# A hybrid decoder block on one core: two value projections and a gate column join pairs that take seven products for eight

## The chip, the cores and the metric

The kernel runs on one core of one Trainium2 chip. The metric is device time in microseconds of one execution. Before the change three runs gave 1403.35, 1406.06 and 1406.92 us; the median, 1406.06 us, is the time before.

## The reference, cut to what matters

One decoder layer on a sequence of 256 tokens with 2048 channels, in float32:

```python
h = rmsnorm(x, g_mix)
proj = h @ w_in                      # 256 x 2048 by 2048 x 12288
q, k, v = ...                        # 16 heads of 128 columns each
gates = sigmoid(proj[..., 3 * MIX_WIDTH:])
o_a = stick_breaking_attention(q[:, :4], k[:, :4], v[:, :4])
qn = rmsnorm(q[:, 4:], q_gain); kn = rmsnorm(k[:, 4:], k_gain)
o_b = moba_attention(qn[:, :6], kn[:, :6], v[:, 4:10], rel_bias[:, :6])
o_c = dilated_attention(qn[:, 6:], kn[:, 6:], v[:, 10:], rel_bias[:, 6:])
merged = gates[0] * (o_a @ w_branch[:512]) + gates[1] * (o_b @ ...) + gates[2] * (o_c @ ...)
x = x + merged @ w_out
gu = rmsnorm(x, g_ffn) @ w_gu
return x + (silu(gu[..., :5632]) * gu[..., 5632:]) @ w_down
```

The change touches the columns of `w_in` for v and for one gate, and the norms and attentions that lie among those projections. The sixteen heads are worked in four groups of four: group 0 is the stick-breaking one, groups 1 to 3 are softmax groups with a norm on q and k.

## The kernel before, in words

**Products.** Every float32 matmul of a projection is made from three float32r products of a high and a low part (`product`, lines 174 to 178): high by high, high by low, low by high. So each 128 x 1024 block of weights is split once: ACT casts it to `w_hi`, DVE subtracts that from the block and writes `w_lo` (`split`, line 110). `w_hi` and `w_lo` have five buffers each; the blocks arrive by DMA in four buffers `w_raw` and six `g_raw`.

**Units.** The first projection is worked as a list of units, each of one or two column blocks of 512. A plain unit (`project`) takes 16 row blocks by 2 token tiles by 3 products, that is 96 matmuls and 8 splits. A pair (`project_pair`) computes two column blocks at once. For half of the rows (the chunks `WC`) it uses seven block products where eight would do (Strassen-Winograd: sums of blocks of the activations are made beforehand, sums of blocks of the weights, `u` and `g_raw`, are made on DVE at lines 320 and 331), and for the other half it works plainly. That makes 180 matmuls, 22 splits, 8 sums of blocks on DVE, four copies of intermediate results out of PSUM on ACT (`snapshot`, line 315) and four 128 x 512 sums on DVE that give the results (lines 375, 377, 380, 389). A form of the seven takes six products from each split, a plain step twelve.

**Order.** The units before are v0, gate, qk0, qk1, v1, qk2, v2, qk3, v3, gate, and then five pairs of gate columns. The qk units and the gate pairs are pairs; v0 to v3 and two gate columns are plain. Everything else lies among them as generators that are advanced step by step: `stages` at each split, `slow_stages` at each second one. `rows_to_columns` squares q and k with sums per row on ACT (line 663, 16 per group), makes the inverse root on DVE and ACT, scales the rows on DVE (line 681), and turns them: groups 0 to 2 by PE transposes, group 3 by DMA transposes issued from ACT between two copies (lines 650, 652 and 673). `attention` then runs two pairs of heads per group; for a softmax pair the scores (lines 591, 593) go to DVE and ACT for the softmax, come back to PE as transposes (618 to 620), are copied to `pT` on ACT (621), and meet v on PE (628, 629); ACT copies the result out (544). `keep_v` finishes all slow stages before it takes the single buffer of v, so one group's attention has to end before the next v.

The kernel's instructions pass through a scheduler that orders each engine's queue by its own estimate of time; a step given to `keep_in_program_order` keeps its place among the others so marked. Each engine then runs its queue in that order.

**Later work.** After the group attentions the pool of the attention is closed, two further PSUM banks come free for the pairs (`acc2`, `beside`), and the attention's output is split (`split_o`) at four given places. Branch projections, output projection, the two products of the feed-forward part follow.

Of the kernel before, what the change touches and what calls it, by code (L numbers as in the profile page):

```python
# [18 lines left out]
P = 128  # L19
# [38 lines left out]
def hybrid_block(ctx: ExitStack, tc: tile.TileContext, x, w_in, w_branch, w_out, w_gu, w_down, rel_bias, xT, gains,  # L58
# [132 lines left out]
            nc.vector.tensor_scalar(t, t, -0.5, 1.5, op0=ALU.mult, op1=ALU.add)  # L191
            nc.vector.tensor_mul(dst if it else y, y, t)

    def transpose4(src):

        pt = tr.tile([P, 4, P], F32, name="tr")
        for i in range(4):
            nc.tensor.transpose(pt[:, i, :], src[:, i * P:(i + 1) * P], ident)
        return pt


# [454 lines left out]
    def rows_to_columns(g, sbs, dst):  # L656
        if g:
            ss = pa.tile([P, 4 * NT * 2], F32, name="ss", bufs=1)
            for i, sb in enumerate(sbs):
                junk = half_kb()  # L660
                for hd in range(4):
                    cols = slice(hd * HD, (hd + 1) * HD)
                    nc.scalar.activation(junk[:, cols], sb[:, cols], AF.Square,
                                         accum_out=ss[:, 4 * i + hd:4 * i + hd + 1])
                yield
            rr = pa.tile([P, 4 * NT * 2], F32, name="rr", bufs=1)
            rsqrt_mean(rr, ss, HD, 4 * NT * 2)
            yield
        def join(d, turned, j):
            joined.append(j)  # L670
            if j == 0 and g:
                turned = turned[..., ::-1]
            tc.keep_in_program_order(nc.scalar.copy(d.bitcast(U16).rearrange("p k (q b) -> p b k q", b=2), turned))
            if j == 0 and g:
                hs = 4 * g - H_A
                nc.vector.tensor_mul(d, d, gq[:, hs:hs + 4, None].to_broadcast([P, 4, P]))

        for i, sb in enumerate(sbs):
            if g:
                sb3 = sb.rearrange("p (h d) -> p h d", h=4)  # L680
                nc.vector.tensor_mul(sb3, sb3, rr[:, 4 * i:4 * i + 4, None].to_broadcast([P, 4, HD]))
                yield
            j, t = divmod(i, NT)
            if g not in (3,):
                pt = transpose4(sb)
                d = dst[j][:, :, t * P:(t + 1) * P]
                if j:
                    nc.scalar.copy(d, pt)
# [12 lines left out]

    def until_joined(g):
# [26 lines left out]
    heads = {}  # L729

    def keep_v(g, ps):
        if g:
            finish_stages(slow_stages)
        heads["v", g] = v = pa.tile([P, NT, NB], F32, name="v", bufs=1)

        def scaled():
            for t in range(NT):
                nc.scalar.activation(v[:, t, :], ps[t], AF.Copy, scale=rstd[:, t:t + 1])
            yield

        if g:
            finish_stages([scaled()])
            slow_stages.append(until_joined(g))
            slow_stages.append(attention(g, *heads["qk", g], v))
        else:
            stages.extend((first_norm(), scaled()))

    def keep_qk(g, q0, q1, k0, k1):
        sbs = []
# [8 lines left out]
        if g:  # L758
            stages.append(rows_to_columns(g, sbs, qkT))
        else:  # L760
            slow_stages.append(rows_to_columns(g, sbs, qkT))
            slow_stages.append(attention(g, *qkT, heads["v", g]))

    chunks = [(c, b) for c in range(4) for b in range(3)]
# [6 lines left out]
    def pair_of(kind, what):  # L773
        if kind == "qk":
            return hs, w_in, what * NB, NH * HD + what * NB
        if kind == "gates":
            return hs, w_in, gate_col(*what[0]), gate_col(*what[1])

    def in_turn():
        turn.reverse()  # L780
# [8 lines left out]
    others = in_turn  # L789
    ahead = None  # L790
    for (kind, what), after in zip(units, units[1:] + [(None, None)]):
        if kind == "gates" and what[0] == chunks[4]:
            finish_stages(slow_stages)
            pat.close()
            acc2 = ctx.enter_context(tc.tile_pool(name="acc2", bufs=1, space=PSUM))
            others = beside
            o = Columns(pool(ph1, "o", "left"), "o", NH)
            for i in range(NH // 4):
                at_split[split_count[0] + 22 * i + 12] = [lambda k=4 * i: split_o(k)]
        nxt = pair_of(*after)  # L800
        if kind in ("qk", "gates"):
# [7 lines left out]
        finish_stages(stages)  # L809
        if kind == "v":  # L810
            keep_v(what, ps)
        elif kind == "qk":
            keep_qk(what, *ps)
        elif kind == "gate":
            keep_gate(*what, ps)
        else:
# [336 lines left out]
```

## Time and profile before

| | |
|---|---|
| median of three runs | 1406.06 us (1403.35 to 1406.92) |
| span of the profiled execution | 1402.7 us |
| PE busy | 1394.4 us, 99%, 6197 instructions |
| DVE busy | 1208.7 us, 86%, 1290 instructions |
| ACT busy | 959.1 us, 68%, 1204 instructions |
| weight loads of PE busy | 1150.2 us, 82% |
| HBM traffic | 220 GB/s over the span |

The profiled execution's own time is its span, 1402.7 us from the first to the last instruction; the runs' times contain what lies around that, and their median is 3.4 us longer. Engines are PE (matmul), PEld (its weight loads), DVE, ACT, POOL and SP. A matmul's end is modelled: a matmul of 512 columns is shown with about 0.39 us but the next one starts about 0.227 us later, so that a wait of PE under some 0.16 us does not show as idle time.

### The profile page before, as it was taken

The numbers are of one execution on the slowest core, as the hardware profiler recorded it, in microseconds if no ns is written. First come the engines' busy times: TensorE is split into PE (matmuls) and PEld (weight loads), VectorE is DVE, ScalarE is ACT, GpSimd is POOL, SyncE is SP. The second block draws the span as 40 slices with busy tenths as digits, with TensorE's granted clock in tenths as the row PEclk, the third lists the DMA queues.
The fourth block names the chain that finished last, engine by engine and source line by source line (L and its number), as shares of the span: only waits on it lengthen the run. The fifth ranks groups of instructions, "written<-read, shape, count | busy, mean of one in ns | idle before, by whom it ended". The sixth has DMA issues, their size and how long they took to land. (4 is left out here: it accounts for less than half of the span.)

```text
span 1402.7 us, 17407 instructions
## 1 busy us (share of the span) xinstructions
PE 1394.4 (99%) x6197; PEld 1150.2 (82%) x6197; DVE 1208.7 (86%) x1290; ACT 959.1 (68%) x1204; POOL 20.1 (1%) x45
## 2 busy tenths in 40 slices
PE   9999999999999999999999999999999999999998
PEld 7888888888888888888878888888888888788887
DVE  6997887857899997875789999999999998997887
ACT  7777867787767675666767677776776776754553
POOL 1000000000000000000000000000000000000000
PEclk9999999999999999999999999999999999999999
DMA  9764647684657667998876766677877779877562
GB/s 341 277 225 125 235 123 251 182 228 137 235 202 246 223 200 264 326 278 243 263 232 239 225 205 222 205 210 250 250 234 240 231 226 307 281 239 260 196 198 87
DMA packets 208967, 320.56 MB, mean 229 GB/s; under 512 B 53064, under 2 KB 65376, under 8 KB 208880
## 3 DMA queue, kind: packets, MB, share of 16 engines
q1 hardware_dynamic: 153216, 293.64, 62.8%
q10 hardware_dynamic: 53136, 17.86, 6.6%
q0 software_dynamic: 2528, 7.95, 1.5%
q8 instruction: 48, 0.79, 0.2%
q14 instruction: 39, 0.32, 0.1%
HBM read 294.22 MB, written 14.70 MB: 220 GB/s over the span
## 5 line engine op out<-in xcount | busy, mean ns | idle before, releaser
L110 DVE TENSOR_TENSOR w_lo<-w_raw,w_hi 128x1024 fp32r<-128x1024 f32 x324 | 393.0, 1220 | 96.9 <-ACT w_hi L110 95.3
L110 ACT CAST w_hi<-w_raw 128x1024 fp32r<-128x1024 f32 x324 | 337.2, 1050 | 107.1 <-PE qs L178 29.5
L110 ACT CAST w_hi<-g_raw 128x1024 fp32r<-128x1024 f32 x192 | 199.8, 1052 | 110.4 <-PE ps L178 38.1
L110 ACT CAST w_hi<-u 128x1024 fp32r<-128x1024 f32 x144 | 151.5, 1053 | 150.2 <-DVE u L320 75.5
L110 DVE TENSOR_TENSOR w_lo<-g_raw,w_hi 128x1024 fp32r<-128x1024 f32 x192 | 228.8, 1220 | 25.4 <-ACT w_hi L110 24.3
L110 DVE TENSOR_TENSOR w_lo<-u,w_hi 128x1024 fp32r<-128x1024 f32 x144 | 172.2, 1220 | 19.0 <-ACT w_hi L110 13.7
L177 PE MATMUL ps<-w_lo,h_hi 128*128 128x512 f32 x352 | 137.5, 391 | 0.0
L178 PE MATMUL ps<-w_hi,h_lo 128*128 128x512 f32 x352 | 137.3, 390 | 0.0
L176 PE MATMUL ps<-w_hi,h_hi 128*128 128x512 f32 x352 | 131.2, 390 | 0.0
L177 PE MATMUL qs<-w_lo,h_hi 128*128 128x512 f32 x332 | 129.8, 391 | 0.0
L178 PE MATMUL qs<-w_hi,h_lo 128*128 128x512 f32 x332 | 129.3, 390 | 0.0
L176 PE MATMUL qs<-w_hi,h_hi 128*128 128x512 f32 x332 | 124.6, 394 | 0.0
L320 DVE TENSOR_TENSOR u<-u,g_raw 128x1024 f32<-128x1024 f32 x80 | 94.4, 1219 | 0.0
L177 PEld LDWEIGHTS ps<-w_lo,h_hi 128*128 128x128 f32 x352 | 66.1, 188 | 13.8
L178 PEld LDWEIGHTS ps<-w_hi,h_lo 128*128 128x128 f32 x352 | 66.1, 188 | 13.6
L176 PEld LDWEIGHTS ps<-w_hi,h_hi 128*128 128x128 f32 x352 | 65.9, 188 | 13.6
L178 PEld LDWEIGHTS qs<-w_hi,h_lo 128*128 128x128 f32 x332 | 62.3, 188 | 13.0
L176 PEld LDWEIGHTS qs<-w_hi,h_hi 128*128 128x128 f32 x332 | 62.3, 188 | 12.8 <-issue 0.2
L177 PEld LDWEIGHTS qs<-w_lo,h_hi 128*128 128x128 f32 x332 | 62.4, 188 | 12.7
L331 DVE TENSOR_TENSOR u<-g_raw 128x1024 f32<-128x1024 f32 x40 | 48.7, 1219 | 10.7 <-DMA g_raw<-in_w_in 9.5
L320 DVE TENSOR_TENSOR g_raw<-g_raw 128x1024 f32<-128x1024 f32 x40 | 47.1, 1218 | 0.0
L177 PE MATMUL v<-w_lo,h_hi 128*128 128x512 f32 x120 | 46.9, 390 | 0.0
(400 smaller groups left out, 2933.1 us busy)
## 6 DMA issues: line engine op xcount, KB each, us to landing
w_raw<-in_w_in SPq DMA_DIRECT2D x116, 512.0 KB, 4.8
g_raw<-in_w_gu SPq DMA_DIRECT2D x88, 512.0 KB, 5.5
w_raw<-in_w_gu SPq DMA_DIRECT2D x88, 512.0 KB, 5.9
g_raw<-in_w_in SPq DMA_DIRECT2D x72, 512.0 KB, 5.7
w_raw<-in_w_down SPq DMA_DIRECT2D x56, 512.0 KB, 5.3
w_raw<-in_w_branch SPq DMA_DIRECT2D x32, 512.0 KB, 5.9
w_raw<-in_w_out SPq DMA_DIRECT2D x32, 512.0 KB, 4.7
g_raw<-in_w_down SPq DMA_DIRECT2D x32, 512.0 KB, 5.3
```

What stands on the lines that cost most here:

```text
L110: for op in nc.scalar.copy(hi, src), nc.vector.tensor_sub(lo, src, hi.bitcast(F32)):
L176: nc.tensor.matmul(ps, ah, wh, start=start, stop=False, **how)
L177: nc.tensor.matmul(ps, ah, wl, start=False, stop=False, **how)
L178: nc.tensor.matmul(ps, al, wh, start=False, stop=stop, **how)
L320: tc.keep_in_program_order(nc.vector.tensor_add(d, d, a))
L331: nc.vector.tensor_add(d, a, b)
```

## The change

Four things are changed in the code.

- The units are now v0, gate, qk0, qk1, the pair vv (v1 with v2), qk2, qk3, the pair vg (v3 with a gate column), and then the same five pairs of gate columns. Four plain units have become two pairs.
- v has two buffers (`bufs` left at the pool's 2), `keep_v` no longer finishes the slow stages, and `attend` appends a group's attention: group 1 after vv, group 2 after qk2, group 3 after vg. `mark` and `finish_heads` hold groups apart.
- The squares, the scaling of the rows, and the transposes of groups 1 to 3 are kept in program order; the scaling steps are three advances apart for groups 1 and 2; group 3's joins are 12 splits behind, not 8, with one advance between.
- The attention's pool is closed one gate pair later (before chunk 6, not chunk 4), and `split_o` steps are 16 splits apart, not 22.

```diff
-    def transpose4(src):
+    def transpose4(src, pin=False):
...
-                    nc.scalar.activation(junk[:, cols], sb[:, cols], AF.Square,
-                                         accum_out=ss[:, 4 * i + hd:4 * i + hd + 1])
+                    tc.keep_in_program_order(nc.scalar.activation(
+                        junk[:, cols], sb[:, cols], AF.Square, accum_out=ss[:, 4 * i + hd:4 * i + hd + 1]))
...
-                nc.vector.tensor_mul(sb3, sb3, rr[:, 4 * i:4 * i + 4, None].to_broadcast([P, 4, HD]))
+                tc.keep_in_program_order(nc.vector.tensor_mul(
+                    sb3, sb3, rr[:, 4 * i:4 * i + 4, None].to_broadcast([P, 4, HD])))
                 yield
+                if g < 3:
+                    yield
+                    yield
...
-            behind(split_count[0] + (8 if g else 6), join, dst[j][:, :, t * P:(t + 1) * P], turned, j)
-            for _ in range(2 if g else 2):
-                yield
+            behind(split_count[0] + 12, join, dst[j][:, :, t * P:(t + 1) * P], turned, j)
+            yield
...
     def keep_v(g, ps):
-        if g:
-            finish_stages(slow_stages)
-        heads["v", g] = v = pa.tile([P, NT, NB], F32, name="v", bufs=1)
+        heads["v", g] = v = pa.tile([P, NT, NB], F32, name="v")
...
+    def attend(g):
+        slow_stages.append(until_joined(g))
+        slow_stages.append(attention(g, *heads["qk", g], heads["v", g]))
+        slow_stages.append(mark(g))
...
-    units = [("v", 0), ("gate", chunks[0]), ("qk", 0), ("qk", 1), ("v", 1), ("qk", 2), ("v", 2), ("qk", 3), ("v", 3)]
-    units += [("gate", chunks[1])] + [("gates", chunks[i:i + 2]) for i in range(2, len(chunks), 2)]
+    units = [("v", 0), ("gate", chunks[0]), ("qk", 0), ("qk", 1), ("vv", (1, 2)), ("qk", 2), ("qk", 3),
+             ("vg", (3, chunks[1]))]
+    units += [("gates", chunks[i:i + 2]) for i in range(2, len(chunks), 2)]
...
-        if kind == "gates" and what[0] == chunks[4]:
+        if kind == "gates" and what[0] == chunks[6]:
...
-                at_split[split_count[0] + 22 * i + 12] = [lambda k=4 * i: split_o(k)]
+                at_split[split_count[0] + 16 * i + 8] = [lambda k=4 * i: split_o(k)]
...
+        elif kind == "vv":
+            finish_heads(0)
+            for i, g in enumerate(what):
+                keep_v(g, ps[NT * i:NT * (i + 1)])
+            attend(1)
+        elif kind == "vg":
+            finish_heads(1)
+            keep_v(what[0], ps[:NT])
+            keep_gate(*what[1], ps[NT:])
+            attend(3)
```

In the built programs PE has 24 matmuls fewer, DVE 36 two-operand instructions more (12 splits, 16 sums of blocks, 8 sums of results), ACT 20 copies more (12 casts, 8 snapshots). The loads of activation tables are 16 in both. The first 509 rows of PE and its last 3858 rows, which begin in the last gate pair, read the same in both, so that what differs lies between the unit qk1 and that pair.

**ACT, at the start of the unit after qk1.** In these rows `w_hi` are casts of weights, line 663 (now 665) the squares of q and k of group 1, 557 (now 559) the logarithm of the stick-breaking group, 755 (now 772) the copies of q and k out of the unit qk1. Ahead of them stand the copy out of the stick-breaking group's first pair (line 544, now 546) and the absolute value of its second (555, now 557). Before, the unit is the plain v1:

```order
L556 ACTIVATE p<-p 128x768
L557 ACT_TABLE_LOAD
L557 ACTIVATE p<-p 128x768
L110 CAST w_hi<-w_raw 128x1024
L755 ACTIVATE sc<-qs,rstd 128x512
L755 ACTIVATE sc<-sc,rstd 128x512
L110 CAST w_hi<-w_raw 128x1024
L663 ACTIVATE sc,ss<-sc 128x128 x16
L110 CAST w_hi<-w_raw 128x1024 x2
```

Now, where the unit is the pair vv:

```order
L110 CAST w_hi<-u 128x1024
L772 ACTIVATE sc<-qs,rstd 128x512
L772 ACTIVATE sc<-sc,rstd 128x512
L558 ACTIVATE p<-p 128x768
L110 CAST w_hi<-u 128x1024
L317 COPY sc<-ps 128x512
L110 CAST w_hi<-w_raw 128x1024
L665 ACTIVATE sc,ss<-sc 128x128 x5
L559 ACT_TABLE_LOAD
L559 ACTIVATE p<-p 128x768
L665 ACTIVATE sc,ss<-sc 128x128 x3
L110 CAST w_hi<-w_raw 128x1024
```

The squares of group 1 and the logarithm of group 0 stood among the casts of a plain unit; they stand now among the casts of a pair's first forms, with a snapshot (line 317) more.

**PE, where a softmax pair's transposes are followed by its product with v.** `tr<-ident,p` are the transposes of the softmax weights, `att<-kT,qT` scores, `tr<-pT,v` the product with v. Before, at the start of qk3:

```order
L618 MATMUL tr<-ident,p 128x128
L619 MATMUL tr<-ident,p 128x128
L620 MATMUL tr<-ident,p 128x128
L591 MATMUL att<-kT,qT 128x256 x2
L593 MATMUL att<-kT,qT 128x128 x2
L628 MATMUL tr<-pT,v 128x256
L629 MATMUL tr<-pT,v 128x128
```

Now, in the second half of vg, for the second pair of group 2:

```order
L620 MATMUL tr<-ident,p 128x128
L621 MATMUL tr<-ident,p 128x128
L622 MATMUL tr<-ident,p 128x128
L620 MATMUL tr<-ident,p 128x128
L621 MATMUL tr<-ident,p 128x128
L622 MATMUL tr<-ident,p 128x128
L630 MATMUL tr<-pT,v 128x256
L631 MATMUL tr<-pT,v 128x128
```

Nothing stands any more between the transposes and the product that needs the copies of them.

**ACT, where group 3 is turned by DMA.** Lines 650 and 673 (now 652 and 675) are the copies on both sides of the DMA transposes (652, now 654), 738 (now 741) the copies of v, 726 (now 731) the sigmoid of a gate. Before, this stands in the plain unit v3:

```order
L650 COPY sc<-sc 128x1024 x2
L652 DMA_TRANSPOSE sc<-sc 128x8x128 x2
L650 COPY sc<-sc 128x1024 x2
L110 CAST w_hi<-w_raw 128x1024
L673 COPY qT<-sc 128x2x4x128
L110 CAST w_hi<-w_raw 128x1024
L544 COPY o_raw<-tr 128x512
L738 ACTIVATE v<-ps,rstd 128x512
L652 DMA_TRANSPOSE sc<-sc 128x8x128 x2
L738 ACTIVATE v<-ps,rstd 128x512
L110 CAST w_hi<-w_raw 128x1024
L673 COPY qT<-sc 128x2x4x128
```

Now, at the end of the pair vg, after the copy out of group 2 (line 546), twice two copies of line 652 with a snapshot and the first two DMA transposes between them, a cast, and the first copy of line 675:

```order
L654 DMA_TRANSPOSE sc<-sc 128x8x128 x2
L110 CAST w_hi<-g_raw 128x1024 x2
L675 COPY qT<-sc 128x2x4x128
L110 CAST w_hi<-g_raw 128x1024 x2
L675 COPY kT<-sc 128x2x4x128
L741 ACTIVATE v<-qs,rstd 128x512
L110 CAST w_hi<-u 128x1024
L731 ACT_TABLE_LOAD
L731 ACTIVATE sc<-sc,rstd 128x512 x2
L741 ACTIVATE v<-sc,rstd 128x512
L110 CAST w_hi<-u 128x1024
L675 COPY kT<-sc 128x2x4x128
```

The same steps have moved from a plain unit to the passage from one pair to the next, and the sigmoid with its table load stands among them.

More of the change, by code (lines that the diff above doesn't have):

```diff
@@ L192, in rsqrt_mean @@
             nc.vector.tensor_mul(dst if it else y, y, t)
-    def transpose4(src):
+    def transpose4(src, pin=False):
         pt = tr.tile([P, 4, P], F32, name="tr")
         for i in range(4):
-            nc.tensor.transpose(pt[:, i, :], src[:, i * P:(i + 1) * P], ident)
+            op = nc.tensor.transpose(pt[:, i, :], src[:, i * P:(i + 1) * P], ident)
+            if pin:
+                tc.keep_in_program_order(op)
         return pt
@@ L680, in rows_to_columns @@
                 sb3 = sb.rearrange("p (h d) -> p h d", h=4)
-                nc.vector.tensor_mul(sb3, sb3, rr[:, 4 * i:4 * i + 4, None].to_broadcast([P, 4, HD]))
+                tc.keep_in_program_order(nc.vector.tensor_mul(
+                    sb3, sb3, rr[:, 4 * i:4 * i + 4, None].to_broadcast([P, 4, HD])))
                 yield
+                if g < 3:
+                    yield
+                    yield
             j, t = divmod(i, NT)
             if g not in (3,):
-                pt = transpose4(sb)
+                pt = transpose4(sb, g > 0)
                 d = dst[j][:, :, t * P:(t + 1) * P]
@@ L742, in keep_v, with mark, finish_heads @@
             finish_stages([scaled()])
-            slow_stages.append(until_joined(g))
-            slow_stages.append(attention(g, *heads["qk", g], v))
         else:
             stages.extend((first_norm(), scaled()))
+    def attend(g):
+        slow_stages.append(until_joined(g))
+        slow_stages.append(attention(g, *heads["qk", g], heads["v", g]))
+        slow_stages.append(mark(g))
+    done = []
+    def mark(g):
+        done.append(g)
+        return
+        yield
+    def finish_heads(g):
+        while g not in done:
+            advance(slow_stages)
     def keep_qk(g, q0, q1, k0, k1):
@@ L777, in pair_of @@
             return hs, w_in, gate_col(*what[0]), gate_col(*what[1])
+        if kind == "vv":
+            return hs, w_in, V0 + what[0] * NB, V0 + what[1] * NB
+        if kind == "vg":
+            return hs, w_in, V0 + what[0] * NB, gate_col(*what[1])
     def in_turn():
@@ L798, in hybrid_block @@
             for i in range(NH // 4):
-                at_split[split_count[0] + 22 * i + 12] = [lambda k=4 * i: split_o(k)]
+                at_split[split_count[0] + 16 * i + 8] = [lambda k=4 * i: split_o(k)]
         nxt = pair_of(*after)
-        if kind in ("qk", "gates"):
+        if kind in ("qk", "gates", "vv", "vg"):
             ps, ahead = project_pair(*pair_of(kind, what), ahead, nxt)
@@ L811, in hybrid_block @@
             keep_v(what, ps)
+        elif kind == "vv":
[8 more added lines that the diff above has]
+            attend(3)
         elif kind == "qk":
+            if what == 3:
+                finish_heads(1)
             keep_qk(what, *ps)
+            if what == 2:
+                attend(2)
         elif kind == "gate":
```

1 line of the change is left out of this document (added).

## The prediction

> **What bounds the kernel now.** I read the page first, then the busy time by stretches, then the engines' timelines in the stretch that the change touches, and last the waits.
>
> ```profile
> span 1402.7 us, 17407 instructions
> PE 1394.4 (99%) x6197; PEld 1150.2 (82%) x6197; DVE 1208.7 (86%) x1290; ACT 959.1 (68%) x1204; POOL 20.1 (1%) x45
> ```
>
> PE is the bound. Counting 180 matmuls for a pair and 96 for a plain unit along PE's row, qk1 begins at 91.60 us, the second gate pair ends at 418.96 and the fifth, the last, at 541.36. The first stretch below is thus qk1 to the second gate pair, five pairs and four plain units with the attention among them; the second is three gate pairs without attention.
>
> ```profile
> core 0: us, PE busy (x) PEld busy (x) DVE busy (x) ACT busy (x) POOL busy (x), PEclk, DMA share, GB/s
> 91.60:418.96 327.36, 326.74 (x1514) 270.95 (x1513) 264.83 (x316) 238.90 (x395) 3.24 (x6) 1.00 0.60 190
> 418.96:541.36 122.40, 122.40 (x542) 101.35 (x541) 112.12 (x104) 81.57 (x92) 6.49 (x12) 1.00 0.65 218
> ```
>
> The second stretch has 540 products in 122.40 us, 0.2267 us each, at full clock (1.00) and without a gap, though DVE works 112.12 of them (92%). In the first, 1284 products would take 291.0 us; the 228 other matmuls (156 of 128 columns at 0.109, 68 of 256 at 0.215, 4 of 512 at 0.428, the pitches in the rows below) take 33.3. So 324.4 of 327.36 us are work and about 3.0 us are waits, of which the page shows 0.62 as idle. The two largest are these:
>
> ```profile
> 384.22 0.39 PE L176 MATMUL z<-w_hi,b_shi 128*128 128x512 f32 x1
> 384.99 0.50 PE L177 MATMUL z<-w_lo,b_shi 128*128 128x512 f32 x1 [0.38 <-DVE w_lo L110]
> ...
> 240.56 1.03 PE L198 MATMUL tr<-ident,sc 128*128 128x128 f32 x8
> 241.83 0.33 PE L618 MATMUL tr<-ident,p 128*128 128x128 f32 x1 [0.24 <-ACT kT L688]
> ...
> 242.10 0.27 PE L620 MATMUL tr<-ident,p 128*128 128x128 f32 x1
> ...
> 242.41 0.97 ACT L621 COPY pT<-tr 128x384 f32<-128x384 f32 x2
> ...
> 242.70 1.03 PE L591 MATMUL att<-kT,qT 128*128 128x256 f32 x4
> 243.57 0.61 PE L593 MATMUL att<-kT,qT 128*128 128x128 f32 x4
> 244.01 0.60 PE L628 MATMUL tr<-pT,v 128*128 128x256 f32 x2
> ```
>
> From start to start the first lost 0.77 less 0.23, 0.54 us; the second 1.27 less eight transposes of 0.109, 0.40. The last rows show a handover: the ACT copy starts 0.31 us after the start of the transpose it needs, 0.2 past that one's pitch, and 1.31 us of scores fill PE until v is multiplied. Four matmuls of 256 columns take 0.87 us, four of 128 columns 0.44.
>
> **The change, part by part.** All sums are made against the span of 1402.7 us; the median of the runs is 3.4 us above it, and I add that at the end. A difference under 0.3%, 4.2 us, cannot be told from none here.
>
> *Products.* Two pairs of 180 matmuls replace four units of 96: 24 matmuls less, 24 x 0.2267 = 5.44 us less PE work. Nothing hides PE, so this is a gain unless waits eat it. With all 3.0 us of waits gone too it would be 8.4, which is the most that the stage can give.
>
> *What is added.* DVE gets 36 instructions, 28 of 1024 elements and 8 of 512; ACT gets 12 casts and 8 snapshots. The prices, back to back, are read from these rows:
>
> ```profile
> 239.63 2.35 DVE L110 TENSOR_TENSOR w_lo<-w_raw,w_hi 128x1024 fp32r<-128x1024 f32 x2
> ...
> 289.45 0.30 ACT L663 ACTIVATE sc<-sc 128x128 f32<-128x128 f32 x1
> ...
> 294.15 1.98 ACT L110 CAST w_hi<-w_raw 128x1024 fp32r<-128x1024 f32 x2
> 296.15 1.28 ACT L185 ACT_TABLE_LOAD   x1
> 297.44 0.22 ACT L185 ACTIVATE rs_y<-rs_v 128x16 f32<-128x16 f32 x1
> ...
> 312.89 1.26 ACT L738 ACTIVATE v<-ps,rstd 128x512 f32<-128x512 f32 x2
> 314.04 1.05 ACT L110 CAST w_hi<-w_raw 128x1024 fp32r<-128x1024 f32 x1
> ...
> 318.39 1.04 ACT L110 CAST w_hi<-w_raw 128x1024 fp32r<-128x1024 f32 x1
> 319.33 1.35 ACT L673 COPY kT<-sc 128x1024 uint16<-128x1024 uint16 x1
> 320.56 1.03 ACT L110 CAST w_hi<-g_raw 128x1024 fp32r<-128x1024 f32 x1
> ...
> 336.95 0.58 ACT L315 COPY sc<-ps 128x512 f32<-128x512 f32 x1
> 337.43 2.00 ACT L110 CAST w_hi<-w_raw 128x1024 fp32r<-128x1024 f32 x2
> ```
>
> Two splits take DVE 2.35 us of which the last's 1.22 is not pitch: 1.13 each. A cast on ACT takes 0.95 (318.39 to 319.33), a join of group 3 1.23, a copy of v 0.575, a snapshot 0.48, a table load 1.29, and the 16 squares of a group 4.70 us (289.45 to 294.15), 0.294 each. So DVE gets 28 x 1.13 + 8 x 0.60 = 36.4 us and ACT 12 x 0.95 + 8 x 0.48 = 15.2. Put on the first stretch and one gate pair, that is 368 us, DVE stands at 93% in place of 82% and ACT at 78% in place of 72% (busy time of the rows above, a gate pair's third of the second stretch added). On the mean both fit; a loss can only come where they bunch.
>
> *Where ACT bunches.* A cast can run at most five buffers ahead of PE, and ACT runs its queue in order. I count ACT's work between two points of PE's order that it depends on, with nothing for its idle time, so each is a lower bound of its delay. Behind a late cast are queued ACT's later casts, and DVE's low part and PE's products wait for it.
>
> First, the start of vv. From the end of the stick-breaking pair's product with v to the first product that reads the eighth split of vv PE has 43 products, 9.75 us. ACT has the handover 0.2, the copy out 0.48, three passes of 768 columns 2.25 (estimate: mean 0.85 in the row below less the overlap), four casts 3.8, two copies 1.15, a snapshot 0.48, eight squares 2.35, a table load 1.29 and 0.1 back, 12.1 us in all. PE waits 2.4. Before, the same squares stood in a plain unit, which uses a cast in 2.72 us of PE; a form uses one in 1.36.
>
> ```profile
> L557 ACT ACTIVATE p<-p 128x768 f32<-128x768 f32 x2 | 1.7, 848 | 0.0
> ```
>
> Second, the start of qk3, where group 2's squares stand as eight and eight around a snapshot and a copy. From the end of the first form to the first product with the fifth split's low part PE has 37 products and three transposes, 8.71 us. ACT and DVE have 0.2, two snapshots 0.96, three casts 2.85, 16 squares 4.70, a copy 0.37, then DVE's 1.13 and 0.2 for handovers: 10.4. PE waits 1.7.
>
> Third, the end of vg. PE's transposes and the product with v now follow each other: the first copy ends 0.9 us after the third transpose starts, PE has 0.43 of transposes to fill that, and loses 0.45, where 1.31 of scores stood before. From the end of that product to the first scores of group 3 PE has 78 products, 17.7 us. ACT has a handover and the copy out, 0.68, then this, as in the old v3:
>
> ```profile
> 303.57 1.99 ACT L650 COPY sc<-sc 128x1024 uint16<-128x1024 uint16 x2 [0.47 <-DVE sc L681]
> 304.65 2.71 ACTq L652 DMA_TRANSPOSE sc<-sc  x2
> 307.39 1.99 ACT L650 COPY sc<-sc 128x1024 uint16<-128x1024 uint16 x2 [1.83 <-DVE w_lo L110]
> ```
>
> ACT stands until its queue has issued both DMA transposes, so four copies take 3.82 + 1.9 = 5.7 us (a snapshot goes into the gap). Then seven casts 6.65, four joins 4.92, two copies of v and two sigmoids 2.3, a table load 1.29: 21.5 us with the first 0.68. PE waits 3.8.
>
> *A rule on the table loads.* The row is 296.15 to 297.44: cast end to load start 0.02, load start to next activation 1.29. The Trainium skill, "ScalarE: Activation LUTs", section "What ACT_TABLE_LOAD costs", adds a drain of about 1.38 us to each switch, 2.66 us in total. By it the first and the third place would each lose 1.38 more, and the change would end slower. No such time stands in the rows, so the sum goes without it.
>
> *What goes.* The waits of 0.54 and 0.40 stand at steps that are taken apart: 0.94 us. The waits ahead of row 509 of PE's order stay, 0.6. The rest, 1.4, I leave as it is.
>
> *At nothing.* The second v buffer frees ACT of a wait that PE does not show. Loads keep their number and size; they land 4.8 us after issue and a pair's buffers are 7 us ahead, and DMA is busy 60% there. If that cover went, one load's 4.8 us would show. SP's and POOL's other transfers (bias, gates) are moved, none added. The four splits of the attention's output cost the same 4 x 1.13 on DVE at pairs of 92%.
>
> *Sum.* -5.44 + 2.4 + 1.7 + 0.45 + 3.8 - 0.94 = +2.0 us: 1404.7 by the span, 1408 beside the median.
>
> **The rivals.**
>
> *All 24 products show.* If ACT's delay is hidden, because it starts each bunch earlier than I count, the gain is 5.44 to 6.4 us: 1400.6 to 1399.7. For it: ACT is at 68%. Against it: the bunches are counted without idle time. Chance 0.14.
>
> *DVE becomes the bound in qk3 and vg.* By the built order DVE has there 62 instructions of 1024 elements (70.1), 8 sums of results (4.8) and 16.5 of norms and softmax, 91.4 us, while PE has 360 products and 10.2 of attention, 91.8. Any idle time of DVE then counts, from the point where its lead is used up: four buffers of 8.2 products, 7.4 us.
>
> ```profile
> DVE w_lo L110 <- ACT w_hi L110: 133.3, 142, 4.2
> ```
>
> Over the kernel's 660 splits DVE waits 133.3 us for casts, 0.20 each, 8.9 us in 44 splits. The loss is 1.2 us if the lead is whole at the start and 8.9 if the delay at the start of qk3 has used it up; in the middle 5, so 1413. Against it: the gate pairs of the second stretch run without a gap at 92%. Chance 0.30.
>
> *The drain of the rule above.* Two loads at 1.38 more, 1410.8; its chance, by the rows, 0.03.
>
> That the change doesn't do what it says is excluded by the count of 24 matmuls.
>
> **How the numbers follow.** The likeliest is the sum, 1408.0, within 0.3% of 1406.06 (1401.8 to 1410.3), chance 0.53; its own range, with one of the three places wrong by its price either way, is 1404 to 1412. Faster by over 0.3% has the first rival's 0.14, slower the other two's 0.33. The range 1401.0 to 1413.5 takes in the middle of the DVE case and leaves out the first rival and the upper tail.
>
> **What would show it.** PE with 6173 matmuls; at the start of vv a product with a high part waiting on ACT for about 2.4 us, at the start of qk3 one of 1.7, at the first scores of group 3 waits that sum to 3.8 behind line 675. If PE's idle time between qk1 and the last gate pair is below 2 us, the bunches are wrong. If the waits end at DVE with ACT long done, DVE is the bound.

## The result, and the profile after

After: 1412.68 us, the median of four runs (1412.21 to 1415.07). Before, on the same chip: 1406.49 us (1403.35 to 1407.93). The ratio is 1.0052, with a 95% interval of 1.0036 to 1.0067: the change costs 6.2 us. The forecast of no difference was wrong; 1412.7 us lies at the upper end of its range. The profiled execution took 1415.07 us, 2.4 us above the median, so that waits read from it are, if anything, larger than the median's.

The page of after, span and engines:

```profile
span 1413.0 us, 17426 instructions
PE 1394.4 (99%) x6173; PEld 1146.5 (81%) x6173; DVE 1241.8 (88%) x1326; ACT 973.9 (69%) x1224; POOL 20.1 (1%) x45
```

The 24 matmuls are gone, and PE is busy for as long as before: something made others longer. By stretches, the first from qk1 to the second gate pair, then four short ones:

```profile
core 0: us, PE busy (x) PEld busy (x) DVE busy (x) ACT busy (x) POOL busy (x), PEclk, DMA share, GB/s
91.91:428.42 336.51, 326.70 (x1489) 268.17 (x1488) 298.35 (x352) 253.56 (x414) 3.25 (x6) 0.99 0.56 187
149.70:152.30 2.60, 0.38 (x2) 0.00 (x0) 1.76 (x2) 2.60 (x9) 0.00 (x0) 0.95 0.51 182
152.30:155.50 3.20, 3.17 (x7) 2.43 (x8) 3.20 (x6) 2.89 (x18) 0.00 (x0) 0.50 0.13 9
323.25:326.60 3.35, 0.38 (x2) 0.00 (x0) 2.61 (x6) 2.48 (x3) 0.00 (x0) 0.93 0.07 23
326.60:329.50 2.90, 2.85 (x7) 2.27 (x8) 1.98 (x3) 1.55 (x2) 0.00 (x0) 0.50 0.77 174
```

The first stretch took 327.36 us and takes 336.51. In the second row PE stands; in the third it works, but the granted clock (the first number behind the engines, 0.50) is half. The fourth and fifth repeat the pair. PE's waits in the first stretch (who waited, for whom, us in all, times, longest), where before there were 0.62 us of idle time in that stretch:

```profile
PE qs L176 <- ACT sc L317: 3.0, 1, 3.0
PE qs L176 <- ACT w_hi L110: 2.6, 2, 2.3
PE ps L177 <- DVE w_lo L110: 2.1, 3, 0.8
PE att L593 <- ACT kT L675: 0.7, 1, 0.7
PE qs L177 <- DVE w_lo L110: 0.6, 1, 0.6
```

**The start of vv.** PE's timeline there:

```profile
149.69 0.39 PE L178 MATMUL qs<-w_hi,h_lo 128*128 128x512 f32 x1
152.33 1.27 PE L176 MATMUL qs<-w_hi,h_hi 128*128 128x512 f32 x2 [2.26 <-ACT w_hi L110]
153.40 0.63 PE L177 MATMUL qs<-w_lo,h_hi 128*128 128x512 f32 x1
153.83 0.63 PE L178 MATMUL qs<-w_hi,h_lo 128*128 128x512 f32 x1
```

From start to start the wait is 2.64 less 0.23, 2.4 us: the forecast's first term, to the tenth. But then the products follow each other at 0.43 us (153.40 to 153.83) in place of 0.227, and over the next seven steps another 1.6 us is lost, which stands in no term.

**The end of vg.** PE, ACT and DVE:

```profile
323.23 0.40 PE L178 MATMUL qs<-w_hi,h_lo 128*128 128x512 f32 x1
326.65 0.80 PE L176 MATMUL qs<-w_hi,h_hi 128*128 128x512 f32 x1 [3.02 <-ACT sc L317]
```

```profile
321.59 0.59 ACT L546 COPY o_raw<-tr 128x512 f32<-128x512 f32 x1 [1.28 <-PE tr L631]
324.12 1.99 ACT L652 COPY sc<-sc 128x1024 uint16<-128x1024 uint16 x2 [1.95 <-DVE sc L683]
326.02 0.58 ACT L317 COPY sc<-qs 128x512 f32<-128x512 f32 x1
```

```profile
302.10 0.18 DVE L189 TENSOR_TENSOR rs_t<-rs_y 128x16 f32<-128x16 f32 x1
...
307.47 0.17 DVE L191 TENSOR_SCALAR rs_t<-rs_t 128x16 f32<-128x16 f32 x1
...
323.19 0.17 DVE L192 TENSOR_TENSOR rr<-rs_y,rs_t 128x16 f32<-128x16 f32 x1
323.40 2.50 DVE L683 TENSOR_TENSOR sc<-sc,rr 128x512 f32<-128x512 f32 x4
```

Start at the last of these views. Behind the exponential on ACT, the norm's inverse root is a chain of eight DVE steps of 0.17 us, each needing the one before. The first starts at 302.10, the last at 323.19: 21 us for 1.4 us of work, because the scheduler puts splits, sums of blocks and softmax steps between them. So the row scalings (683) are late; ACT's copies for the DMA transposes (652) wait 1.95 us for them at the head of ACT's queue; the snapshot (317), which needs nothing of that, stands behind them; and PE waits 3.2 us for the snapshot, with 1.4 us more at half clock. DVE's wait is thus 1.95 us of the 3.2; the two copies and the snapshot take the rest. During that chain DVE is busy for 20.6 of 21.5 us. Before, the same chain lay in the plain unit v3, in which DVE is busy for 13.5 of 22.3 us:

```profile
300.16 0.17 DVE L189 TENSOR_TENSOR rs_t<-rs_y 128x16 f32<-128x16 f32 x1 [0.30 <-ACT rs_y L186]
...
302.63 0.18 DVE L192 TENSOR_TENSOR rr<-rs_y,rs_t 128x16 f32<-128x16 f32 x1
302.85 2.50 DVE L681 TENSOR_TENSOR sc<-sc,rr 128x512 f32<-128x512 f32 x4
```

**The balance.** From qk1's first product to the end of the gates before took 449.76 us, after 459.65: 9.9 more in these two executions. Each matmul's start to the next one's start, less its pitch (0.227 us for a product), adds up to what PE lost, half clock included: 17.7 us against 2.4, and 15.3 - 5.44 = 9.9. Outside the stage both take the same (861.3 and 861.4 us behind it). In detail after: vv 2.4 and 1.6; start of qk3 2.1; vg 0.4, 0.5, 0.46, 0.8, 3.2 and 1.4; group 3's scores 1.0; the start of the second gate pair 1.0; the rest in pieces under 0.6.

### The profile page after: what moved, and what is told of

Read it like the earlier page. It is cut to its first block, busy times and chain, and to the rows that moved or that the text cites. A ratio compares the mean times of both kernels' runs of the same rounds, so it can differ in the third digit from the quotient of the medians.

```text
span 1413.0 us, 17426 instructions
## 1 busy us (share of the span) xinstructions
PE 1394.4 (99%) x6173; PEld 1146.5 (81%) x6173; DVE 1241.8 (88%) x1326; ACT 973.9 (69%) x1224; POOL 20.1 (1%) x45
## 5 line engine op out<-in xcount | busy, mean ns | idle before, releaser
L110 DVE TENSOR_TENSOR w_lo<-w_raw,w_hi 128x1024 fp32r<-128x1024 f32 x308 | 373.7, 1221 | 81.4 <-ACT w_hi L110 79.6
L110 ACT CAST w_hi<-w_raw 128x1024 fp32r<-128x1024 f32 x308 | 320.7, 1050 | 88.2 <-DMA w_raw<-in_w_branch 24.8
L110 ACT CAST w_hi<-g_raw 128x1024 fp32r<-128x1024 f32 x208 | 215.9, 1052 | 100.1 <-DVE g_raw L322 30.3
L110 ACT CAST w_hi<-u 128x1024 fp32r<-128x1024 f32 x156 | 164.0, 1053 | 158.9 <-DVE u L322 83.4
L110 DVE TENSOR_TENSOR w_lo<-g_raw,w_hi 128x1024 fp32r<-128x1024 f32 x208 | 247.6, 1221 | 21.3 <-ACT w_hi L110 20.4
L110 DVE TENSOR_TENSOR w_lo<-u,w_hi 128x1024 fp32r<-128x1024 f32 x156 | 186.4, 1221 | 21.3 <-ACT w_hi L110 20.1
L177 PE MATMUL ps<-w_lo,h_hi 128*128 128x512 f32 x328 | 128.4, 391 | 1.1 <-DVE w_lo L110 1.1
L178 PE MATMUL ps<-w_hi,h_lo 128*128 128x512 f32 x328 | 127.7, 389 | 0.0
L176 PE MATMUL ps<-w_hi,h_hi 128*128 128x512 f32 x328 | 120.4, 391 | 0.0
L322 DVE TENSOR_TENSOR u<-u,g_raw 128x1024 f32<-128x1024 f32 x88 | 103.8, 1219 | 0.0
```

The costliest lines, as they stand in the source:

```text
L110: for op in nc.scalar.copy(hi, src), nc.vector.tensor_sub(lo, src, hi.bitcast(F32)):
L176: nc.tensor.matmul(ps, ah, wh, start=start, stop=False, **how)
L177: nc.tensor.matmul(ps, ah, wl, start=False, stop=False, **how)
L178: nc.tensor.matmul(ps, al, wh, start=False, stop=stop, **how)
L322: tc.keep_in_program_order(nc.vector.tensor_add(d, d, a))
```

## The experiments

Theory 1 when they began: ACT's bunches at three places, as predicted, plus the half clock. Theory 2, formed on the way: the chain of small DVE steps. All ratios are to the kernel before, run beside each experiment. The scheduler reorders with every edit, so that no run changes one thing alone, and a time has to be read with its trace. The pins on the squares and on the transposes change nothing: in the built programs the order of every engine is the same without them. The edits are shown cut to their main lines.

**Each pair undone alone.**

```diff
-             ("vg", (3, chunks[1]))]
+             ("v", 3), ("gate", chunks[1])]
```

> The kernel after, with value 3 and gate 1 as two plain projections again (192 products in place of 180, +2.7 us of TensorE), values 1 and 2 still a pair. Nothing is left out. Theory 1 (the losses belong to ScalarE's three bunches): the first two stay (vv 4.1 us, third q/k pair 2.1), that of the last pair goes with its pair (3.2 of wait, 1.4 of half clock, some 2 of small waits), so 1412.7 - 6 + 2.7 = 1409.5 us. Rival (VectorE is the bound in the whole stretch from the third q/k pair on, whose own work the pair adds only six to nine instructions of 0.6 to 1.1 us to): most of the waits stay at the end of the fourth value, 1412.5 us or more.

```diff
-("vv", (1, 2)), ("qk", 2), ("qk", 3),
+("v", 1), ("qk", 2), ("v", 2), ("qk", 3),
```

> The kernel after, with values 1 and 2 as plain projections again, each behind its q/k pair as in the kernel before (+12 products, 2.7 us), value 3 and gate 1 still a pair. Nothing is left out. Theory 1: the start of the first pair loses nothing (-4.1 us), the third q/k pair's start is spared less surely (-1), and the last pair keeps its loss of about 6 us: 1412.7 - 5 + 2.7 = 1410.4 us, and with the run that undoes the other pair the two differences from the kernel after add up to the 6.2 us between the two kernels. Rival (the loss at the end belongs to what vv piles up ahead of it, in VectorE's and ScalarE's arrears, and not to the last pair): the waits at the end go too, and the time comes under 1406 us.

Ratios 1.0055 [1.0040, 1.0071] and 1.0084 [1.0064, 1.0104]. Neither undoing helps, and the two don't add up: theory 1 failed both, and so did the rival of the second run, which promised less than 1406 us against 1414.7. Without the pair vg, group 3's DMA transposes fell into a burst of loads (DMA share 1.00 to 1.21); issuing them took 5.9 us (two), 3.5 and 3.2, and ACT stood for up to 5 us; without vv, the wait at the snapshot (2.1 us, ACT behind its copies 652) and two more at the start of the next pair remained. So undoing one pair does not take away the loss at the end of the stretch.

**The third part alone, and the pairs without it.**

```diff
                 yield
+                if g < 3:
+                    yield
+                    yield
```

> The kernel before, without any pair of values, with only the change's third part: the row scalings of groups 1 to 3 pinned, two more steps behind each row of groups 1 and 2, group 3's joins twelve steps behind their transposes in place of eight, with one step between its rows in place of two. Nothing is left out. Theory 1 (the losses come from the shorter stretch of products that the same work of ScalarE has to lie beside): no change, within 1.5 us of the kernel before. Rival (the order of the norm's steps is itself the loss, which is why undoing either pair alone left the time at the kernel after's): +5 to +9 us.

> The kernel after with both pairs, and the steps of the norm and of group 3's turn as in the kernel before: no pins, no further steps, joins eight steps behind, two steps between rows. Nothing is left out. Theory 1 (the pairs squeeze the work): the bunches at the two starts stay as they are, 4.1 and 2.1 us; group 3's copies, two steps apart, no longer stand side by side ahead of the snapshot, which may spare up to 3 us; +3 to +7 us on the kernel before. Rival (the order of the steps is the loss): the waits go, and the time comes to the kernel before's less the 5.4 us of the 24 products, -5 to -2 us.

1.0068 [1.0050, 1.0085] and 1.0111 [1.0092, 1.0130]. In the kernel before the new steps cost about 9.5 us, a little over the rival's size: 6.4 us are lost in qk3 and 5.6 in the gate unit behind v3, there with a wait of 3.2 us after three DMA transposes have held ACT for 11 us. But the pairs with the old steps are the slowest run of all, 15.6 us above, where the rival promised a gain and theory 1 a loss of 3 to 7 us. So the steps' order is worth as much as the pairs, and which order is better depends on the units beside it; the new one fits the pairs and repairs a part of what they break.

**ACT's squares later.**

```diff
+            for _ in range(3 if g < 3 else 0):
+                yield
             for i, sb in enumerate(sbs):
```

> The kernel after, with the squares of groups 1 and 2 begun three steps (of about 2.7 us) later, so that in ScalarE's order the casts of the first weights stand ahead of them at the start of the pair of values 1 and 2 and of the third q/k pair. Nothing is left out. Theory 1 (ScalarE's bunches at these two starts cost what the waits there show): the 2.4 us, the half clock's 1.7 us behind it and the 2.1 us at the start of the third q/k pair go, 1406.5 to 1408.5 us. Rival (VectorE sets the pace from there to the end of the fourth value): the two waits go, but what they took comes back as waits for VectorE's w_lo or its row scalings later in the same units, above all behind the scalings of group 3, and the time stays within 2 us of 1412.7.

1.0047 [1.0032, 1.0063]. The wait of 2.4 us and its half clock go (0.35 us is left), so ACT's bunch is what made it; 1.7 us come back at 161 to 163 us, and the snapshot keeps its wait of 3.2, now with 6.83 us of half clock behind it. The time theory 1 named, 1406.5 to 1408.5 us, did not come (1411.2); the rival's did. At the snapshot ACT does not wait for DVE in this run: the copy out of group 2, itself late, and the two copies for the DMA transposes stand one behind the other ahead of it.

**ACT's work at the end of vg removed.**

```diff
-            if g not in (3,):
+            if True:
```

> The kernel after, with group 3's q and k turned by 16 TensorE transposes (0.109 us each, 1.7 us), as groups 1 and 2 are, in place of four word-splitting copies (0.95 us), four DMA transposes and four joins (1.23 us) on ScalarE's queue; ScalarE gets two copies of 0.6 us out of PSUM for them, 7.5 us less in all, and VectorE none more than it has. Nothing is left out. Theory 1 (ScalarE's bunch at the end of the pair of value 3 and gate 1 holds the snapshot and the scores up): the 3.2 us of wait at the snapshot, the 1.4 us of half clock behind it and the 1.0 us at group 3's first scores go, 1.7 us of TensorE come: 4 us under the kernel after, +2 us on the kernel before. Rival (VectorE is late there and ScalarE only waits for it: its scalings of the rows end at 325.9 us whichever way the rows are turned): the waits at the end of that pair stay and move to the transposes, and the time is that of the kernel after (+6) or up to 1.7 us above it.

1.0058 [1.0045, 1.0072]: the rival's time, but not for its reason. The wait at the snapshot is gone with the copies; the last pair still loses 8.3 us, against 7.5 in the kernel after. Yet the scalings are not late here: in this order the chain takes 2.7 us, and the first scaling starts at 304.87 us, not at 323.40. PE's transposes stand so close behind it that PE waits for the scalings all the same, and then for casts:

```profile
304.66 0.17 DVE L192 TENSOR_TENSOR rr<-rs_y,rs_t 128x16 f32<-128x16 f32 x1
304.87 0.69 DVE L683 TENSOR_TENSOR sc<-sc,rr 128x512 f32<-128x512 f32 x1
...
305.61 0.66 PE L198 MATMUL tr<-ident,sc 128*128 128x128 f32 x4 [0.53 <-DVE sc L683]
...
309.86 0.79 PE L176 MATMUL qs<-w_hi,b_shi 128*128 128x512 f32 x1 [1.49 <-ACT w_hi L110]
```

So the run shows that neither less work on ACT nor a short chain is enough by itself. Without the pair vg (3.5 us) and in the kernel before with the new steps (4.8 us) the chain is short too, and the time is long.

**DVE's work removed.**

```diff
-            nc.vector.tensor_scalar(p[:, sl], p[:, sl], st[:, 2, j:j + 1], None, op0=ALU.mult)
+            pass
```

> The kernel after without the scaling of the softmax rows by the inverse of their sum (left out, so the outputs of twelve heads are not normalised): four VectorE instructions, 1.0 us, less in each of the six pairs of heads of groups 1 to 3, 6 us of VectorE in all, four of them in the third q/k pair and the pair of value 3 and gate 1, where VectorE is busy for 0.95 of the time. ScalarE and TensorE have the same instructions as in the kernel after. Theory 1 (ScalarE's order sets the waits): within 1.5 us of the kernel after, +5 to +7 us on the kernel before. Rival (VectorE is the bound there): the 4 us come off the stretch, +1 to +3 us.

1.0030 [1.0017, 1.0043], 4.2 us over before: between the two. The chain got shorter as well (15.3 us from the exponential to group 3's first scaling in place of 21.5), so this run can't tell the amount of DVE's work from its order. The next can.

**The chain shortened and lengthened.** `rsqrt_mean` refines twice; here once, in three fused instructions for four, or three times:

```diff
-            rsqrt_mean(rr, ss, HD, 4 * NT * 2)
+            rsqrt_mean(rr, ss, HD, 4 * NT * 2, 1)
```

> The kernel after with one refinement of the q/k norm's inverse root in place of two in groups 1 to 3 (the second is left out, which changes the result at the last digits): four of the nine steps of the chain go, 0.7 us of VectorE per group. Theory 2 (each step of the chain waits for a slot between VectorE's large instructions, about 2.5 us): group 3's scalings come some 10 us sooner, as with the chain on GpSimd, and the time falls by 3 to 6 us, 0 to +3 on the kernel before. Rival (VectorE's amount of work): 0.7 us per group is worth less than 1 us, +5 to +6.

> The kernel after with each refinement in three VectorE instructions in place of four (two of them with a scalar and a second tensor), the same arithmetic: two steps fewer in each chain of groups 1 to 3. Nothing is left out. Theory 2: group 3's scalings come some 4 to 5 us sooner than in the kernel after, and between a third and all of the 4.6 us of wait and half clock at the snapshot goes, 2 to 5 us under the kernel after, +1 to +4 us on the kernel before. Rival (lucky order): within 2 us of the kernel after, +4 to +8.

> The kernel after with three refinements of the q/k norm's inverse root in groups 1 to 3 in place of two: four more steps of 0.17 us on VectorE per group. Nothing is left out. Theory 2 (each small step waits 2 to 2.5 us for its slot between VectorE's large ones, and group 3's scalings, copies, snapshot and scores wait for the last): the scalings of group 3 come some 8 us later than in the kernel after, and the time rises by 3 to 8 us above it, +9 to +14 us on the kernel before. Rival (the run with one refinement fell on a lucky order, the chain's length does not matter): within 2 us of the kernel after, +4 to +8.

The last three columns give what PE lost in the profiled execution, half clock included, in us.

| steps behind the exponential | exponential to group 3's first scaling | ratio | vv | qk3 | vg and first gate pair |
|---|---|---|---|---|---|
| 12 (e13) | 24.1 us | 1.0073 [1.0059, 1.0087] | 4.6 | 1.7 | 10.1 |
| 8 (after) | 21.5 us | 1.0052 [1.0036, 1.0067] | 4.2 | 2.5 | 8.9 |
| 6 (e14) | 17.6 us | 1.0031 [1.0016, 1.0045] | 1.4 | 0.9 | 9.0 |
| 4 (e11) | 10.2 us | 1.0010 [1.0001, 1.0019] | 3.1 | 1.0 | 2.6 |

Four steps fewer, 0.7 us of DVE in each of three groups, are worth 5.9 us, and most of what the trace shows of that is won at the end of vg, where theory 2 puts it. The scalings come at 310.84, and the snapshot's wait is gone from the list of the run with one refinement:

```profile
PE qs L176 <- ACT w_hi L110: 2.3, 1, 2.3
PE ps L177 <- DVE w_lo L110: 1.4, 2, 0.8
PE att L593 <- ACT kT L675: 0.7, 1, 0.7
PE qs L177 <- DVE w_lo L110: 0.5, 1, 0.5
```

The order of the four ratios is what theory 2 says; the intervals of neighbours overlap, the ends don't. But the traces bear it out at the end of vg between eight and four steps only. With six steps the snapshot's wait is gone and one of 2.2 us for a softmax step has come at the transposes; what was won lies in vv, where ACT has another order and PE does not wait, and in qk3. With twelve steps the scalings come at 321.50 us, not some 8 us later as expected, and the time rises by 3 us, the low end of what was expected.

**The chain still shorter, and off DVE.**

```diff
-            nc.vector.tensor_mul(t, y, y)
+            eng.tensor_mul(t, y, y)
```

> The kernel after, with the nine small steps of the q/k norm's inverse root (128x16, 0.17 us each on VectorE) on GpSimd in groups 1 to 3. Nothing is left out. In the kernel after these steps wait in VectorE's queue between its large ones: from the exponential to group 3's first row scaling pass 21.5 us for 1.4 us of work, against 2.9 us in the kernel before. Theory 2 (the loss at the end of the last pair comes from that chain: late scalings, hence a late snapshot or late transposes, hence TensorE): group 3's scalings come some 10 us sooner, the 3.2 us of wait and its 1.4 us of half clock go, the loss at the start of the first pair (4.1 us) stays, some of the 2.1 us at the third q/k pair too: 4 to 6 us under the kernel after, 0 to +2 us on the kernel before. Rival (VectorE's amount of work is what counts): 4 us of small steps are gone from its whole stretch, 1.4 of them in the last pair, and the time falls by no more than 1.5 us, +4.5 to +6 on the kernel before.

> One refinement in three fused steps (the second is left out, which changes the result at the last digits): the chain of each of groups 1 to 3 has three steps behind the exponential in place of eight. Nothing is delayed. If the chain's length sets the loss all the way down: at or up to 2 us under the run with one refinement in four steps, -1 to +1.5 us on the kernel before. Rival (from four steps on another wait ends last): the same as with four steps, +0.5 to +2.5 us.

1.0103 [1.0089, 1.0117] and 1.0006 [0.9994, 1.0017]. The chain on GpSimd takes 3.4 us in group 3, and yet the run is 14.7 us above the kernel before, where theory 2 promised 0 to 2. Both have a new wait at the end of the pair, of 6.6 us with GpSimd and 3.0 with three steps, for a `w_hi` that ACT casts late. ACT with three steps, then with GpSimd (ACTq is ACT's issuing of transfers):

```profile
310.24 1.51 ACTq L653 DMA_TRANSPOSE sc<-sc  x1
...
311.85 5.19 ACTq L653 DMA_TRANSPOSE sc<-sc  x1
317.08 1.05 ACT L651 COPY sc<-sc 128x1024 uint16<-128x1024 uint16 x1 [4.49 <-DVE u L321]
```

```profile
330.09 5.48 ACTq L655 DMA_TRANSPOSE sc<-sc  x2
335.61 1.99 ACT L110 CAST w_hi<-u 128x1024 fp32r<-128x1024 f32 x2 [4.55 <-issue]
```

With the scalings early the transposes are issued while a burst of weights is loading, and ACT, which issues them, is held for about 4.5 us (the releaser shown at 317.08 had long ended). So scalings can come too early as well as too late: with three steps vg and the first gate pair lose 6.2 us, against 2.6 with four. It was not tried with the loads moved.

GpSimd has a price of its own. In group 2 DVE stands 1.9 us for its chain with the splits behind, PE waits 3.1 us for a low part, and half clock for 6.83 us follows; qk3 loses 7.2 us, against 2.5 in the kernel after:

```profile
258.82 0.69 DVE L684 TENSOR_TENSOR sc<-sc,rr 128x512 f32<-128x512 f32 x1 [1.91 <-POOL rr L193]
...
260.71 0.80 PE L177 MATMUL ps<-w_lo,b_shi 128*128 128x512 f32 x1 [3.10 <-DVE w_lo L110]
```

**Both causes at once.**

> The chain on GpSimd as in the run before this one, and the squares of groups 1 and 2 three steps later as in the run with late squares. Nothing is left out. If both mechanisms are right and independent, the 3.4 us that the late squares took off the stage come on top of what the chain's move takes: 8 to 9 us under the kernel after, 1 to 3 us under the kernel before. Rival (each removed wait comes back at the next place, since ScalarE or VectorE has no slack left in the stretch): within 2 us of the better of the two single runs, and not below the kernel before.

> The fused steps and the squares of groups 1 and 2 three steps later. Nothing is left out. If the two causes (squares ahead of casts at the start of the first pair, the long chain ahead of the last pair's end) are right and independent: 3.4 us under the run with fused steps alone, -2 to +1 us on the kernel before. Rival (the late squares make the chain late in turn, so that what is won at the start is lost behind the chain): not better than the fused steps alone.

> One refinement in place of two (the second is left out, which changes the result at the last digits), and the squares of groups 1 and 2 three steps later. If both causes are right and independent: 2.5 to 4 us under the run with one refinement alone, since the wait of 2.4 us and what stands at half clock behind it go: -1 to -3 us on the kernel before, the first version of the pairs to beat it. Rival (no slack is left: the wait comes back at the next weights): within 1 us of the run with one refinement, +0.5 to +2.5.

> One refinement in place of two (the second is left out, which changes the result at the last digits), and the squares of group 1 alone three steps later. If it was group 2's delay that cost e16 what the first delay won: 2 to 3 us under the run with one refinement alone, -1.5 to 0 us on the kernel before. Rival (the wait at the first pair's start only moves to the weights behind it, about 1.7 us at 162 us of e16): within 1.5 us of the run with one refinement.

1.0024 [1.0011, 1.0037], 1.0034 [1.0021, 1.0047], 1.0031 [1.0018, 1.0044] and 1.0000 [0.9990, 1.0010]. Beside the chain on GpSimd the later squares take off 11 us: the first two transposes are then issued in 1.3 us each, and the wait of 6.6 us does not come. To a shorter chain on DVE, later squares in groups 1 and 2 add nothing (with one refinement group 2's first scaling comes at 273.29 us in place of 258.16); in group 1 alone they come out 1.4 us better than the run with one refinement, which the two intervals don't resolve. That best version of the pairs, 1405.71 us against 1405.80, equals the kernel before; it leaves out the second refinement. None beats it. Its waits show why the 5.44 us still don't appear:

```profile
PE ps L177 <- DVE w_lo L110: 2.2, 3, 0.8
PE att L593 <- ACT kT L677: 0.7, 1, 0.7
PE qs L177 <- DVE w_lo L110: 0.5, 1, 0.5
```

**Fillers for the half clock.** Dummy products were to keep PE busy in the waits:

> The kernel after, with 23 dummy products on TensorE (0.227 us each, 5.2 us, into a spare PSUM bank): ten in the pair of values 1 and 2, ahead of its second plain pair of weights, thirteen in the pair of value 3 and gate 1, ahead of its seventh product, the two places where the clock record falls to 0.5 for 3.41 us behind a wait of 2.3 and one of 3.0 us. Nothing is left out. Theory 1 (the half clock is a cost of its own, on top of the wait, and it comes from TensorE standing idle): the dummies lie in the waits of 2.4 and 3.2 us and add next to nothing, the record stays at 1.0 at both places, and the 1.7 and 1.4 us go: 1409.6 us against 1412.7. Rival (ScalarE is short of the time anyway, and the slow products only hide a shortage that would show as a further wait): the waits behind the dummies grow by what the half clock took, and the time stays at 1412.7 or rises by the part of the 5.2 us that no wait covers.

> The kernel after, with ten products of a zero matrix by the last w_lo (0.227 us each, 2.3 us, added into the bank that the next products use, so that nothing changes in it) in the pair of values 1 and 2, right where TensorE waits 2.42 us for w_hi. Nothing is left out. Theory (the half clock comes from TensorE standing idle, and is a cost on top): the cast lands at the same time as before, 152.3 us, the record stays at 1.0 there, and the 1.7 us that products at a pitch of 0.43 us took behind it go: 1.7 us under the kernel after. Rival (the half clock belongs to something else, or the next casts are late by as much anyway): a record of 0.5 at 152 to 156 us all the same, or further waits of 1.7 us for w_hi behind it, and no change.

1.0039 [1.0024, 1.0054] and 1.0063 [1.0049, 1.0076]. Both missed their aim at vv: the scheduler put the products before or behind the wait, which stayed at 2.4 us. The first run's 1410.2 us lies near the 1409.6 that its theory named, but by luck: the half clock at vv stayed, and group 3's scalings happened to come 9.0 us behind the exponential, all eight steps in place, with the snapshot's wait gone. vg lost 0.7 us beside the 3.0 us of its thirteen dummy products. In the second run, with the chain at 21.5 us as in the kernel after, vg lost 8.8. That agrees with theory 2. The two say little on the half clock's cause. In the second it is missing behind the wait at vv, and in the run with one refinement too:

```profile
150.46 0.39 PE L178 MATMUL qs<-w_hi,h_lo 128*128 128x512 f32 x1
153.12 0.98 PE L176 MATMUL qs<-w_hi,h_hi 128*128 128x512 f32 x2 [2.27 <-ACT w_hi L110]
153.94 0.40 PE L177 MATMUL qs<-w_lo,h_hi 128*128 128x512 f32 x1
154.18 0.39 PE L178 MATMUL qs<-w_hi,h_lo 128*128 128x512 f32 x1
```

From 140 to 160 us the run with one refinement loses 2.9 us, the kernel after 4.1.

## Why the prediction was wrong

The forecast counted 7.4 us of new waits against the 5.44 us of the products; the profiled execution has 15.3. Term by term:

- Products, -5.44: right. Added work: right, the counts are those of the page, and DVE is busy for 33.1 us more (36.4 counted) and ACT for 14.8 (15.2).
- Start of vv, 2.4: right in cause and size (2.4, and gone with the squares later).
- Start of qk3, 1.7: 2.1 in three pieces, mostly at `w_lo`.
- Handover at the transposes, 0.45: 0.46.
- End of vg, 3.8: **this step failed.** The sum took group 3's first scores for the place where PE would wait, let a snapshot go "into the gap" of ACT's copies, and counted ACT's queue "with nothing for its idle time", as a lower bound. At the scores (345.73) 1.0 us came. The loss came 19 us ahead of them (326.65), at that snapshot: 3.2 us and 1.4 at half clock, since the snapshot stands behind two copies and ACT stood 1.95 us in front of them, waiting for DVE. With four tiny DVE steps taken out (e11) this wait went, and vg lost 1.2 us in place of 7.5.
- Open in that account: how much belongs to DVE's chain and how much to the copies' place in ACT's queue. With late squares (e2) the snapshot waited as long without ACT waiting for DVE. With the copies taken out (e5) its wait went, the chain was short, and the pair lost as much at other steps.
- Not in the sum: half clock, 1.6 and 1.4; 1.0 at the second gate pair where 0.54 stood; the rest in pieces of up to 0.8.
- "At nothing" should have held the norm's chain. Its eight steps are small, are the same before and after, and so were not counted; what changed is the queue they wait in. The order of DVE shows it: 2.9 us from the exponential to the scalings before, 21.5 after.
- The rival with DVE as the bound gave 1413, the time that came, which is in part luck. Its place was right in the main (qk3 and vg lost 10.0 of the 17.7 us), and so was its engine at the chain, but its mechanism only in part: it added up DVE's work (91.4 us against 91.8), and 4 us less of that was worth about 3 us, while 2 us less of it in the chain was worth 5.9.
- The rule on table loads: load start to next activation is 1.29 us again (340.26 to 341.55), and no drain is seen.

What stays open besides: how the remaining waits in the best version, about 6 us above those before, could go, and whether the half clock would stay away with PE kept busy.

## What to carry to other kernels

Before pairing units, look not only at how much each engine has to do per product, but at chains of small dependent steps on the engine that becomes the fullest: each step waits for a slot, here 1.3 to 5.6 us for 0.17 us of work, and whoever stands behind the chain's consumer in an in-order queue waits too. Then ask what the freed chain will collide with: here several runs with a chain of 3 to 5 us (e3, e5, e6, e9) lost at other places what that chain had spared. A saved matmul counts only where those waits have been removed.

## What the runs showed of the hardware that was not expected

- **A wait costs more than it lasts.** Behind most waits of 2.1 us and more the granted clock fell to 0.5 for 3.41 or 6.83 us, and the products' pitch went from 0.227 to 0.43 us. It is not certain: of ten profiles with the same 2.4 us wait at the start of vv eight have it, two not, and a wait of 2.3 us in e16 has none. Waits of 1.0 us alone never had it; three of 0.8 to 1.1 us within 5 us did (e8). The Trainium skill, "TensorE: Matmul & The Clock Gate", Part 1, says that the clock falls after an idle window of about 3.4 us that runs freely, with no regard to the kernel. The length of 3.41 us agrees, and the chance in it would fit; the idle time needed was less here, 2.3 us of 3.41.
- **Issuing a DMA transpose can hold the issuing engine while the DMA is full.** In the kernel after, at a DMA share of up to 0.84, it took 1.25 to 1.34 us each. At a share of 1.0 to 1.2 one took up to 5.2 us (e18) and three took 11 us (e6), though not each is slow there.
- **The small steps' price on GpSimd varies with what DVE does.** The same 128x16 steps took 0.20 to 0.23 us, or 1.05 to 1.14 us, in one and the same chain. In group 2 of e9 the two slow ones (254.79 and 255.92) lie beside two 128x1024 sums of DVE, the six quick ones behind them where DVE stood. Why was not tested.
